# Two adaLN vector sums moved from the DeltaNet scan to the merge of its output, and the gate stores moved to ACT's queue

## The chip, the cores and the metric

The kernel runs on one core of one Trainium2 chip. The metric is the device time of one execution in microseconds (us). All arithmetic of the reference is float32.

## The reference

One block of a diffusion backbone, over 512 latent tokens and 256 context tokens of width 1024:

```
lat_mod = split(silu(c) @ w_mod + b_mod, 6)
h = rms_norm(x, norm1_g) * (1 + lat_mod[1]) + lat_mod[0]
merged = g_dn * (deltanet(h) @ w_proj_dn) + g_hy * (hyena(h) @ w_proj_hy) + g_lru * (rglru(h) @ w_proj_lru)
x = x + lat_mod[2] * (merged @ w_out)
h = rms_norm(x, norm2_g) * (1 + lat_mod[4]) + lat_mod[3]
x = x + lat_mod[5] * conv_ffn(h)
return rms_norm(x, final_norm_g)
```

The six vectors `lat_mod` (adaLN: shift, scale and gate of the two sub-layers) are a product of one row of 1024 numbers with a 1024 x 6144 matrix. This document is about vectors 2 to 5, called q = 0 to 3 in the kernel: q = 0 scales the output of the mixer, q = 1 and 2 shift and scale the input of the FFN, q = 3 scales its output. The gates g_dn, g_hy and g_lru, and the factor silu(z) of DeltaNet's output, are projections of h.

## The kernel before, in words

The block is one program for one core, and its parts follow each other: norm and modulation of the input, RG-LRU with its merge, queries, keys and values of DeltaNet, the triangular solves, **the scan** (12 steps over chunks of 64 tokens, both directions at once), then **the merge stage**: the first two groups of Hyena's input (`hy_in(0)`, L1143), the norm of DeltaNet's output (`dn_norm`, L1228), eight blocks `dn_merge(m)` (L1251) and Hyena's transform of its first quarter (`hy_fft(0)`, L1166) with its second input (`hy_in(1)`). Then come the rest of Hyena, the output projection and the FFN.

A matrix product is exact to float32 by three passes: each operand is split into a high and a low part, and `mm3` (L172) multiplies high by high (L173), high by low (L174) and low by high (L175). `load_w` (L164) loads a block of weights of 512 KB into a raw buffer (L168, on SP's queue), and `split` (L152) copies the high part (L155 on ACT or L157 on POOL) and subtracts it on DVE or POOL for the low part (L160). There are **three raw buffers** (ring `wr`, 4 KB of every partition each), two for high parts (`wh`) and two for low parts (`wl`), all at L148. Buffers go round: each call takes the next.

In the scan, PE's instructions are kept in the order of the program by `in_order((ET.PE,))` (L1114). A step (L996) subtracts what the state predicts (PE L1025, DVE L1029), applies the solved block (PE L1035, ACT L1037), updates the state (PE L1043, DVE L1048 in 16 pieces) and forms the output (PE L1055, ACT L1058 or DVE L1060). Between the halves of the steps stand 24 halves of 12 gate projections (`gate_halves`, L1091), whose results go through ACT (L594) to DRAM (L595, `gated`). POOL prepares the decayed queries and keys (L1012) from rows loaded at L1007.

Of the four adaLN vectors, `mod_part(q, k)` (L1068) loads 512 KB of w_mod into a raw buffer of the ring `wr` (L1070), multiplies it by c (a number per partition) and adds it to `acc` on DVE (L1072 for k = 0, L1074 for the other seven). `mod_sum(q)` (L1076) adds the partitions by matmuls against ones: eight of one column for q = 1 and 2 (L1080, DVE L1081), two of 512 columns for q = 0 and 3 (L1087, DVE L1088), which are then stored as a row to DRAM (`modr`). Eight products make a vector; in the loop L1103 four of them follow each of the steps 0, 1, 3, 4, 6, 7, 9 and 10, and the sums stand ahead of steps 2, 5, 8 and 11.

`dn_merge(m)` loads a block of `w_proj` by `load_w`, the gate (L1253, `gated[1, m]`) and what is merged so far (L1254, `mgd`), runs 24 matmuls of 512 columns, multiplies by the gate on DVE (L608), adds on POOL (L1256) and stores (L1257). The high part of its weights comes from POOL (L157), the low part from DVE (L160).

Outside the pinned stretches a list scheduler of the framework decides the order of the instructions on each engine and of the DMAs on each queue; engines and queues then run strictly in that order. SP issues nearly all DMAs and itself waits for the buffer that a DMA writes or for the data that it stores.

## Time and profile before

| | us |
|---|---|
| three runs | 2179.06, 1700.55, 1703.49 (median 1703.49) |
| profiled execution | 1699.04, of which 1696.9 span from the first to the last instruction |
| PE busy in the span | 1554.4 (92%) |
| DVE, ACT, POOL busy | 1202.8, 618.8, 587.0 |
| mean granted TensorE clock | 0.957 of full speed |

The sums of this document are made in the profiled execution and then set beside the runs. A matmul's recorded span overlaps that of the next, so a busy PE is not a PE at its peak, and what a change is worth is read from PE's idle time in the stage where it acts. "L160" is line 160 of the kernel before; because the diff takes a line away ahead of them, the lines L1070 to L1088 of `mod_part` and `mod_sum` are L1069 to L1087 after the change, and the merge stage's lines keep their numbers up to its loop.

### The profile page before, as it was taken

To read this page: it belongs to the slowest core of one execution; us is meant where nothing else is said; L and a number is where in the kernel's file an instruction comes from. 1 tells how busy PE (TensorE), PEld (TensorE's weight loads), DVE (VectorE), ACT (ScalarE), POOL (GpSimd) and SP (SyncE) were. 2 spreads that over 40 slices of the span, in tenths; PEclk is the share of its full clock that TensorE was granted. 3 is DMA by queue.
4 is the path that set the end of the run, shared out by engine and by line. 5 is a ranking of instruction groups with operands and counts; after the bars stand their busy time and mean duration, and the time that the engine had idled before them with its cause. 6 is when DMAs were issued, how large, how long until landed. Compare 5 with 4: busy or idle time off the path is not lost. (4 is left out here: it accounts for less than half of the span.)

```text
span 1696.9 us, 23679 instructions
## 1 busy us (share of the span) xinstructions
PE 1554.4 (92%) x9176; PEld 1264.1 (74%) x9176; DVE 1202.8 (71%) x1756; ACT 618.8 (36%) x1014; POOL 587.0 (35%) x407
## 2 busy tenths in 40 slices
PE   6989989889999988987899999999999999999998
PEld 1657767668787766875687777778878788888876
DVE  4677798765655999553675566777665899989873
ACT  3447878753454222231111150332222433333311
POOL 3752444433535351221333313222321234333441
PEclk7989999989999998788999999999999999999999
DMA  8522222234534332467889646322452123232331
GB/s 304 183 93 69 81 74 70 98 111 136 166 108 135 117 92 90 124 196 190 243 238 247 220 173 229 112 87 86 157 191 89 63 87 99 95 104 93 106 112 50
DMA packets 93057, 225.66 MB, mean 133 GB/s; under 512 B 9963, under 2 KB 30699, under 8 KB 92176
## 3 DMA queue, kind: packets, MB, share of 16 engines
q1 hardware_dynamic: 92112, 217.86, 40.9%
q0 software_dynamic: 832, 6.29, 0.9%
q8 instruction: 72, 1.18, 0.3%
q14 instruction: 41, 0.34, 0.1%
HBM read 190.45 MB, written 33.66 MB: 132 GB/s over the span
## 5 line engine op out<-in xcount | busy, mean ns | idle before, releaser
L173 PE MATMUL bank<-region,region 128*128 128x512 f32 (+1 forms) x2032 | 761.4, 376 | 23.8 <-DVE region L507 7.6
L175 PE MATMUL bank<-region,region 128*128 128x512 f32 (+1 forms) x2032 | 755.4, 373 | 24.6 <-DVE region L160 21.3
L174 PE MATMUL bank<-region,region 128*128 128x512 f32 (+1 forms) x2032 | 756.9, 373 | 5.0 <-DVE region L439 2.9
L173 PEld LDWEIGHTS bank<-region,region 128*128 128x128 f32 x2032 | 389.5, 192 | 101.6 <-ACT region L539 9.0
L175 PEld LDWEIGHTS bank<-region,region 128*128 128x128 f32 x2032 | 389.7, 192 | 97.7 <-DVE region L160 27.8
L174 PEld LDWEIGHTS bank<-region,region 128*128 128x128 f32 x2032 | 390.3, 192 | 69.6 <-DVE region L439 4.9
L160 DVE TENSOR_TENSOR region<-region,region 128x1024 fp32r<-128x1024 f32 (+2 forms) x241 | 269.8, 1133 | 173.0 <-ACT region L155 94.9
L155 ACT ACTIVATE region<-region 128x1024 fp32r<-128x1024 f32 (+2 forms) x209 | 178.4, 865 | 427.4 <-PE bank L174 130.0
L160 POOL TENSOR_TENSOR region<-region,region 128x1024 fp32r<-128x1024 f32 (+1 forms) x64 | 155.3, 2431 | 251.2 <-ACT region L155 210.8
L157 POOL TENSOR_SCALAR region<-region 128x1024 fp32r<-128x1024 f32 (+1 forms) x96 | 113.0, 1178 | 337.8 <-PE bank L174 151.2
L1443 DVE SCALAR_TENSOR_TENSOR region<-bank,pc,region 128x441 f32<-128x441 f32 (+2 forms) x352 | 224.8, 688 | 4.3 <-ACT region L1432 0.7
L505 DVE SCALAR_TENSOR_TENSOR region<-bank,pc,region 128x511 f32<-128x511 f32 (+1 forms) x56 | 34.1, 630 | 51.1 <-ACT region L502 47.3
L1074 DVE SCALAR_TENSOR_TENSOR region<-region,cc,region 128x1024 f32<-128x1024 f32 x28 | 42.1, 1504 | 35.9 <-DMA region<-in_w_mod_dram 35.5
L1012 POOL TENSOR_TENSOR region<-region,region 128x512 f32<-128x512 f32 x32 | 45.8, 1460 | 38.3 <-DMA region<-rowd 37.3
L502 ACT ACTIVATE region<-bank,pc 128x512 f32<-128x512 f32 (+1 forms) x40 | 23.0, 597 | 96.2 <-PE bank L175 96.2
L1455 POOL TENSOR_TENSOR region<-region,region 128x512 f32<-128x512 f32 x22 | 34.3, 1560 | 66.1 <-DVE region L1443 52.2
L1048 DVE SCALAR_TENSOR_TENSOR region<-region,egl,bank 128x128 f32<-128x128 f32 x160 | 42.3, 340 | 19.2 <-PE bank L1043 19.2
L1025 PE MATMUL bank<-region,region 128*64 128x128 f32 x608 | 38.9, 287 | 9.4 <-DVE region L1048 9.3
L1025 PEld LDWEIGHTS bank<-region,region 128*64 128x64 f32 x608 | 35.9, 145 | 14.6 <-DVE region L1048 6.3
L1037 ACT ACTIVATE region<-bank 128x512 f32<-128x512 f32 x24 | 14.3, 598 | 88.1 <-PE bank L1035 87.7
L594 ACT ACTIVATE region<-bank 128x512 f32<-128x512 f32 x32 | 18.8, 587 | 70.1 <-PE bank L175 66.0
L1035 PE MATMUL bank<-region,region 64*64 64x128 f32 x384 | 28.3, 298 | 12.7 <-DVE region L1029 6.9
(286 smaller groups left out, 1697.1 us busy)
## 6 DMA issues: line engine op xcount, KB each, us to landing
region<-in_w_in_dram SPq DMA_DIRECT2D x97, 512.0 KB, 3.6
region<-in_w_mod_dram SPq DMA_DIRECT2D x48, 512.0 KB, 6.7
region<-in_ffn_up_dram SPq DMA_DIRECT2D x44, 512.0 KB, 3.5
region<-in_w_proj_dram SPq DMA_DIRECT2D x24, 512.0 KB, 3.7
region<-in_ffn_down_dram SPq DMA_DIRECT2D x22, 512.0 KB, 3.4
gated<-region SPq DMA_DIRECT2D x32, 256.0 KB, 2.1
region<-gated SPq DMA_DIRECT2D x32, 256.0 KB, 3.5
kdd<-region SPq DMA_DIRECT2D x16, 384.0 KB, 2.8
```

The source lines that it names most:

```text
L155: act(hi, raw, AF.Copy)
L157: nc.gpsimd.tensor_scalar(hi, raw, 1.0, 0.0, op0=ALU.mult, op1=ALU.add)
L160: (vtt if e_lo == "dve" else gtt)(lo, raw, hi.bitcast(F32), op=ALU.subtract)
L173: mmul(ps, lh, rh, start=start, stop=False)
L174: mmul(ps, lh, rl, start=False, stop=False)
L175: mmul(ps, ll, rh, start=False, stop=stop)
L1012: gtt(wq[d][:, hs], KQ[hf][:, :, chs[d] - 4], eg[:, hs].unsqueeze(2).to_broadcast([P, 4, 2, 64]), op=ALU.mult)
L1025: mmul(X[hf][rcs[d], h, :], wq[d][:, hf * 4 + h, kind], S[d][:, hf * 4 + h, :], start=(kind == 0 or h == 0), stop=(kind == 0))
L1048: stt(S[d][:, h], S[d][:, h], egl[:, d, c, i, h:h + 1], p3[hf][d][:, h % 4], op0=ALU.mult, op1=ALU.add)
L1074: stt(acc, w_, cc[:, k, 0:1], acc, op0=ALU.mult, op1=ALU.add)
L1443: stt(uv[:, ro, co], pv_[:, ri, ci], w[:, a * 3 + b:a * 3 + b + 1], uv[:, ro, co], op0=ALU.mult, op1=ALU.add)
L1455: gtt(uu[0], uu[0], uu[1], op=ALU.mult)
```

## The change

The products and sums of q = 2 and 3 (16 loads of 512 KB, 16 DVE products, two sums) leave the scan and go into the loop over the eight blocks of the merge: two products behind each `dn_merge(m)`, the sum of q = 2 ahead of block 4, that of q = 3 behind block 7, with an accumulator `acc` of their own at 68 KB. In the scan two products stand behind each of the steps 0 to 3 and 6 to 9, and the sums ahead of steps 5 and 11. The store of a gate in the scan is issued from ACT's queue in place of SP's.

```diff
--- before.py
+++ after.py
@@ -589,10 +589,10 @@
     def load_gate(z_, m, e_hi="pool", e_lo="dve"):
         return load_w(I["w_in"][GATES[z_][0] + m], e_hi=e_hi, e_lo=e_lo)
 
-    def gate_store(z_, m, pg):
+    def gate_store(z_, m, pg, store=load):
         th = ur([P, NL])
         act(th, pg, GATES[z_][1])
-        load(gated[z_, m], th)
+        store(gated[z_, m], th)
 
     def gate(z_, m, e_hi="pool", e_lo="dve"):
         w = load_gate(z_, m, e_hi, e_lo)
@@ -1063,9 +1063,8 @@
 
     modr = dr.tile([2, D], F32, name="modr")
     mod34 = c1([P, 2, 8], "mod34")
-    acc = at(190, [P, D])
-
-    def mod_part(q, k):
+
+    def mod_part(acc, q, k):
         w_ = wr([P, D])
         load(w_, I["w_mod"][k * P:(k + 1) * P, (2 + q) * D:(3 + q) * D])
         if k == 0:
@@ -1073,7 +1072,7 @@
         else:
             stt(acc, w_, cc[:, k, 0:1], acc, op0=ALU.mult, op1=ALU.add)
 
-    def mod_sum(q):
+    def mod_sum(acc, q):
         if q in (1, 2):
             mp = mm([P, 8])
             for b in range(8):
@@ -1093,23 +1092,24 @@
         project_part(w, [(pg, hh, hl)], 0, 4)
         yield
         project_part(w, [(pg, hh, hl)], 4, 8)
-        gate_store(z_, m, pg)
+        gate_store(z_, m, pg, nc.scalar.dma_start)
         yield
 
     first_ins = len(bb.instructions)
     halves = (None for z_, m in fill[NFILL:] for _ in gate_halves(z_, m))
     ngap, FBM = 2 * (24 - NFILL), 1
     gap = 0
+    acc = at(190, [P, D])
     for s_ in range(12):
 
-        if s_ % 3 == 2:
-            mod_sum(s_ // 3)
+        if s_ % 6 == 5:
+            mod_sum(acc, s_ // 6)
         for part, _ in enumerate(step(s_)):
             gap += 1
             for _ in range(gap * ngap // 24 - (gap - 1) * ngap // 24):
                 next(halves)
-        for k in range(4) if s_ % 3 < 2 else ():
-            mod_part(s_ // 3, s_ % 3 * 4 + k)
+        for k in range(2) if s_ % 6 < 4 else ():
+            mod_part(acc, s_ // 6, s_ % 6 * 2 + k)
     assert next(halves, 1) == 1
     in_order((ET.PE,))
     dump("o", o)
@@ -1259,8 +1259,15 @@
 
     hin = hy_in(0)
     dn_norm()
-    for m in range(8):
+    acc = at(68, [P, D])
+    for m in range(9):
+        if m and m % 4 == 0:
+            mod_sum(acc, 1 + m // 4)
+        if m == 8:
+            break
         dn_merge(m)
+        for k in range(2):
+            mod_part(acc, 2 + m // 4, m % 4 * 2 + k)
         if m == FBM:
             nc.gpsimd.dma_start(fb, I["c_fwd"])
         if m == FBM + 1:
```

Three places show what that does to the order. In all rows region_902, region_440 and region_720 are the three raw weight buffers, region_721 and region_441 the two buffers for high parts, region_722 and region_442 those for low parts.

The first is DVE's queue in the merge stage, from the gate product (L608) of block 4 on. Before:

```order
L608 TENSOR_TENSOR region_1515<-region_1515,bank_64 128x512
L160 TENSOR_TENSOR region_722<-region_902,region_721 128x1024
L608 TENSOR_TENSOR region_974<-region_974,bank_65 128x512
L160 TENSOR_TENSOR region_442<-region_440,region_441 128x1024
L608 TENSOR_TENSOR region_1336<-region_1336,bank_63 128x512
L160 TENSOR_TENSOR region_722<-region_720,region_721 128x1024
```

Now, from the same gate product on (L1071 and L1073 are the products of `mod_part`, region_7297 is `acc`):

```order
L608 TENSOR_TENSOR region_1515<-region_1515,bank_65 128x512
L160 TENSOR_TENSOR region_722<-region_902,region_721 128x1024
L1071 TENSOR_SCALAR region_7297<-region_440,cc 128x1024
L1073 SCALAR_TENSOR_TENSOR region_7297<-region_720,cc,region_7297 128x1024
L160 TENSOR_TENSOR region_442<-region_902,region_441 128x1024
L608 TENSOR_TENSOR region_974<-region_974,bank_63 128x512
L1073 SCALAR_TENSOR_TENSOR region_7297<-region_440,cc,region_7297 128x1024
L1073 SCALAR_TENSOR_TENSOR region_7297<-region_720,cc,region_7297 128x1024
```

Before, the splits of three successive weight blocks read the three raw buffers in turn; now every one reads region_902, and the products read the other two. The gate product of block 5 now stands behind the split of block 7's weights.

The second place is SP's queue from the store of block 4's result (region_1515) to the end of the merge. Before:

```order
L1257 DMA mgd<-region_1515 128x512
L168 DMA region_902<-in_w_in_dram 128x1024
L1253 DMA region_2480<-gated 128x512
L1254 DMA region_1515<-mgd 128x512
L1257 DMA mgd<-region_974 128x512
L168 DMA region_440<-in_w_in_dram 128x1024
L1254 DMA region_974<-mgd 128x512
L1257 DMA mgd<-region_1336 128x512
L168 DMA region_720<-in_w_in_dram 128x1024
L1257 DMA mgd<-region_2480 128x512
```

Now, from the store of block 6's result (region_1336) on:

```order
L1257 DMA mgd<-region_1336 128x512
L1253 DMA region_2480<-gated 128x512
L1254 DMA region_974<-mgd 128x512
L1069 DMA region_440<-in_w_mod_dram 128x1024
L1069 DMA region_720<-in_w_mod_dram 128x1024
L1257 DMA mgd<-region_2480 128x512
L1083 DMA region_440<-in_b_mod_dram 1x1024
L168 DMA region_720<-in_w_in_dram 128x1024
```

Before, the gate of block 7 (the only L1253 of its piece) was issued ahead of the store of block 5's result, and the weights of `hy_in(1)` (in_w_in) stood among the blocks; now the gate of a block follows the store of the block before it, and the first weights of `hy_in(1)` stand behind the last store and in a buffer that the last product reads.

The third is PE's queue at the end of `hy_fft(0)` (bank_69). Before, `hy_in(1)` follows at once:

```order
L173 MATMUL bank_69<-region_7038,region_106 128x256
L174 MATMUL bank_69<-region_7038,region_106 128x256
L175 MATMUL bank_69<-region_7038,region_106 128x256
L173 MATMUL bank_65<-region_80,region_721 128x512
L174 MATMUL bank_65<-region_81,region_721 128x512
```

Now the sum of q = 3 (L1086) and two pieces of `hy_out(0)` (weights region_744) stand between:

```order
L174 MATMUL bank_69<-region_6991,region_106 128x256
L175 MATMUL bank_69<-region_6991,region_106 128x256
L1086 MATMUL bank_63<-region_7297,ones 1x512
L1086 MATMUL bank_64<-region_7297,ones 1x512
L173 MATMUL bank_67<-region_744,region_7869 128x256
L174 MATMUL bank_67<-region_744,region_7869 128x256
L173 MATMUL bank_68<-region_744,region_7869 128x256
L174 MATMUL bank_68<-region_744,region_7869 128x256
L173 MATMUL bank_65<-region_80,region_721 128x512
```

Of the 48 matmuls of 256 columns of `hy_fft(0)`, 21 are now spread over the blocks of the merge, and 27 stand between block 7 and L1086; before, all 48 stood behind block 7.

## Rows read from the trace of the kernel before

**Rows 1.** Busy time by stage: us; engines (instructions); granted clock; DMA share; GB/s
```profile
764.00:975.00 211.00, 183.88 (x1928) 151.58 (x1928) 118.11 (x236) 30.97 (x61) 62.62 (x50) 0.94 0.81 227
1030.00:1063.00 33.00, 32.37 (x143) 26.76 (x144) 17.36 (x13) 1.10 (x2) 13.29 (x11) 1.00 0.72 248
1063.00:1069.00 6.00, 6.00 (x51) 5.96 (x50) 5.59 (x7) 2.22 (x3) 1.29 (x1) 1.00 0.48 160
```

**Rows 2.** PE's waits in the scan, 780 to 970 us: total, times, longest
```profile
PE bank L1025 <- DVE region L1048: 9.3, 4, 5.9
PE bank L1035 <- DVE region L1029: 6.9, 5, 3.5
```

**Rows 3.** Timeline at scan step 3: start, us, engine, line [idle before <-releaser]
```profile
809.81 1.28 DVE L1074 SCALAR_TENSOR_TENSOR region<-region,cc,region 128x1024 f32<-128x1024 f32 x1
...
811.12 0.65 SPq L168 DMA_DIRECT2D region<-in_w_in_dram  x1
...
817.66 1.04 POOL L157 TENSOR_SCALAR region<-region 128x1024 fp32r<-128x1024 f32 x1 [5.12 <-DMA region<-in_w_in_dram]
818.74 1.22 DVE L160 TENSOR_TENSOR region<-region,region 128x1024 fp32r<-128x1024 f32 x1 [2.89 <-POOL region L157]
...
820.54 3.68 PE L1025 MATMUL bank<-region,region 128*64 128x128 f32 x32 [5.92 <-DVE region L1048]
```

**Rows 4.** Timeline of PE at the adaLN sums, and L1025 at scan step 2
```profile
800.12 1.02 PE L1087 MATMUL bank<-region,ones 128*1 128x512 f32 x2 [0.69 <-ACT region L594]
801.91 1.02 PE L1087 MATMUL bank<-region,ones 128*1 128x512 f32 x2 [0.77 <-DVE region L1088]
802.87 1.97 PE L1025 MATMUL bank<-region,region 128*64 128x128 f32 x32
...
853.08 1.95 PE L1080 MATMUL bank<-ones,region 128*128 128x1 f32 x16 [0.69 <-ACT region L594]
...
956.48 1.02 PE L1087 MATMUL bank<-region,ones 128*1 128x512 f32 x2 [0.69 <-ACT region L594]
959.24 1.53 PE L1087 MATMUL bank<-region,ones 128*1 128x512 f32 x2 [1.74 <-DVE region L1088]
```

**Rows 5.** Granted clock around the stall of step 3, columns as in the first group
```profile
802.80:804.80 2.00, 2.00 (x35) 1.75 (x34) 1.37 (x2) 0.00 (x0) 0.73 (x1) 1.00 0.49 127
820.50:824.30 3.80, 3.68 (x32) 3.28 (x32) 3.77 (x3) 0.00 (x0) 3.20 (x2) 0.50 0.76 195
```

**Rows 6.** SP's waits in the scan, 780 to 970 us
```profile
SPq L595 <- ACT region L594: 29.8, 10, 8.5
```

**Rows 7.** Timeline of one block of the merge: DVE, POOL and SP
```profile
1041.32 1.05 POOL L157 TENSOR_SCALAR region<-region 128x1024 fp32r<-128x1024 f32 x1 [1.54 <-issue]
1041.43 0.69 DVE L608 TENSOR_TENSOR region<-region,bank 128x512 f32<-128x512 f32 x1 [3.24 <-PE bank L175]
1042.34 1.28 POOL L1256 TENSOR_TENSOR region<-region,region 128x512 f32<-128x512 f32 x1
1042.41 2.30 DVE L160 TENSOR_TENSOR region<-region,region 128x1024 fp32r<-128x1024 f32 x1 [0.29 <-POOL region L157]
1044.29 0.36 SPq L1257 DMA_DIRECT2D mgd<-region  x1
1044.74 0.39 SPq L168 DMA_DIRECT2D region<-in_w_in_dram  x1
1046.88 0.69 DVE L608 TENSOR_TENSOR region<-region,bank 128x512 f32<-128x512 f32 x1 [2.17 <-PE bank L175]
```

**Rows 8.** DMAs issued in the merge, 1010 to 1066 us: KB each, median us to landing
```profile
region<-gated SPq DMA_DIRECT2D x12, 256.0 KB, 2.9
region<-in_w_proj_dram SPq DMA_DIRECT2D x4, 512.0 KB, 3.8
```

**Rows 9.** DMAs issued in the scan, 760 to 970 us
```profile
region<-in_w_mod_dram SPq DMA_DIRECT2D x27, 512.0 KB, 5.6
```

**Rows 10.** DVE's adaLN products: ns shortest, median, longest
```profile
L1074 DVE SCALAR_TENSOR_TENSOR region<-region,cc,region x28: 1272/1285/2267, 747.8 to 944.8; 128x1024 f32<-128x1024 f32 x28
```

## The prediction

> **What bounds the kernel now.** I read the page's slices first, then the busy time by stage, then, stage by stage, what PE waits for and the timeline there. By stage [rows 1], PE is busy 183.88 of 211 us in the scan, so some 27 us are idle, 5 of them at its start; DVE's 118.11 us show that the 16 products which leave were not too much work, only in the way. In the merge PE is busy 32.37 of 33 us: there is nothing to win there, and each wait that comes in is lost. So the change moves work from a stage with holes into a full one, and the question is which waits go and which come.
>
> In the scan PE waits 9.3 us for DVE's state update (L1048) and 6.9 us for its subtraction (L1029) [rows 2]. The longest of these, 5.92 us ahead of step 3, shows the mechanism [rows 3]: the adaLN product ends at 811.09, only then does SP issue the next gate's weights (811.12) into the buffer that it freed, POOL gets them at 817.66, DVE's split stands in its queue ahead of the last two update pieces and ends at 819.96, and PE goes on at 820.54. The two long matmul sums also hold PE up themselves [rows 4].
>
> **Gain in the scan.** (a) The sums. Before, with their waits: at step 2 0.69+1.02+0.77+1.02 = 3.50 us, at steps 5 and 8 0.69+1.95 = 2.64 each, at step 11 0.69+1.02+1.74+1.53 = 4.98 [rows 4] (the sum at step 8 read the same as that at step 5); 13.8 us. Now one of the first kind and one of the second stay, 6.1 us. Gain 7.6 us.
> (b) The waits for DVE, 9.3 + 6.9 = 16.2 us [rows 2]. With half the products, gate weights no longer share their raw buffer with a product, so the stall of rows 3 should go; those where the update merely stood behind products should shrink. But each split still stands ahead of a step's subtraction. I take two thirds, 11 us; bounds 3 and 16.2. A loss isn't excluded, since every gate's weights now use one buffer, but a gate is due only about every 17 us (211/12) and its load, 5.6 us in this stage [rows 9], fits.
> (c) The clock. Ahead of the stall the granted clock is 1.00 (2.4 GHz), after it 0.50 (1.2 GHz) [rows 5], and the same 32 matmuls take 3.68 us in place of 1.97 [rows 3, 4]. Some of that goes with the stalls: 2.6 us, bounds 0 and 4.3.
> (d) The gate stores. SP stands 29.8 us behind ACT's gate activation [rows 6] with the next step's loads behind it. That wait goes from SP; on ACT the store follows its own producer, and ACT is busy 30.97 of 211 us [rows 1], so it costs nothing there; if that cover failed, 12 issues of 0.4 us would come to 5 us. Its value is in (b), so 0 by itself.
> By the Trainium skill (DMA: Bandwidth & Descriptors, "Issuing engines are not separate DMA queues") a second issuing queue saves only issue time, usually small. Of 11 stores that would be 4 us of SP. Here the row shows waiting on the queue, not issue, as the larger part; by the rule alone (b) would stand nearer its lower bound.
> Sum: 7.6 + 11 + 2.6 = 21 us, bounds 6 and 28.
>
> **Loss in the merge.** A block takes 1046.88 - 1041.43 = 5.45 us now [rows 7].
> (e) The turn of one raw buffer. All w_proj blocks now use region_902, so block m+1 can be loaded only when m's split is done, and the split needs the landing. A turn is landing 3.8 us [rows 8] + POOL 1.05 + DVE 2.30 + 0.2 of hand-overs [rows 7] = 7.35; with two product loads beside it I take 4.05 for the landing: 7.6 us. Bounds: 6.2 with a split of 1.22 [rows 3], 9.2 with the scan's 5.6 [rows 9]. Blocks 0 to 2 have their weights in time. Five turns (blocks 3 to 7) at 7.6 - 5.45 come to 10.8 us; 21 of the transform's matmuls at 6.00/51 = 0.118 us [rows 1] fill 2.5 of that. 8.3 us, bounds 1.3 and 16.3.
> The transfers point the same way: 512 KB of weights, 3 x 256 KB and 2 x 512 KB of w_mod are 2.36 MB a block, and 248 GB/s at a share of 0.72 [rows 1] make 344 GB/s at a full one, or 6.9 us. By the Trainium skill (same page, "Specifications") the limit of HBM is about 358 GB/s per core, an estimate of 6.6 us a block: it speaks against the change, and the trace agrees to 4%.
> (f) The tail. The gate product of block 5 now stands behind the split of block 7's weights, the next gate is loaded only behind a store, and the last products behind that. From that split: L608 0.69, POOL 1.28, hand-overs 0.87, store 0.36 make 3.2 [rows 7]; gate 6 lands 2.9 + 0.1 later [rows 8]; another 3.2 to the store of block 6; 1.3 until both last products' loads are issued behind two others, 5.0 landing (3.8 with company), 1.28 for the last product [rows 10] and 0.2: 17.2 us. PE has block 7 (5.45) and 27 matmuls (3.2) meanwhile: it waits 8.5 us ahead of the sum of q = 3. Bounds: 2, if block 7's split isn't late (PE then has block 6 more), and 14 with the scan's landings.
> (g) The sums themselves: 1.95 and 2 x 1.02 = 4.0 us [rows 4], without a wait between the two, which have banks of their own.
> (h) The weights of `hy_in(1)`. Before, the first was issued at 1044.74 [rows 7], 24 us ahead of its use; now behind the last product, which reads its buffer: 3.8 landing [rows 8], 1.05 for the high part as in rows 7, 1.22 for the low part as in rows 3, hand-overs 0.4 are 6.5 us, of which the sum covers 2.3. 4.2 us, bounds 2 and 6.
> (i) The first of these two gaps is longer than the 5.92 us behind which the clock fell [rows 3, 5], the second shorter; that fall cost 3.68 - 1.97 = 1.7 us [rows 3, 4] and, as I estimate from the same ratio, 0.9 in what followed. 3.5 us for the two, bounds 0 and 5.5.
> The 16 products on DVE (1.29 us each [rows 10], 17.36 of 33 us busy [rows 1]) hide behind the turn; without that cover they would cost at most 21 us, which is inside the upper bounds of (e) and (f).
> Sum: 8.3 + 8.5 + 4.0 + 4.2 + 3.5 = 28.5 us, bounds about 10 and 46.
>
> **Total.** 28.5 - 21.2 = +7.3 us on the profiled execution of 1699.04: 1706.3. Of the runs shown, 1700.55 and the median of 1703.49 lie 3.0 above that execution on the mean, so I predict 1709, practically no change: 2% (34 us, about what a measurement of this kernel can tell from no change) is more than either side.
>
> **Rivals.**
> *The merge absorbs it.* Landings stay at 3.8 us, the splits are short because POOL's addition no longer falls beside them, and block 7's weights come in time: (e) 1.3, (f) 2, (g) 4, (h) 3, (i) 0 = 10 us against 28 in the scan: -18, 1684. For it: DVE and POOL have room in the merge. Against it: the 6.9 us of transfers a block.
> *The merge becomes bound by landings.* At 5.6 us and more, the turn of region_902 is 9.2 us: (e) 16.3, (f) 14, (g) 4, (h) 6, (i) 5.5 = 46 against 15 in the scan: +31, 1733, slower than before. It decides from a turn of about 8 us; over 2% from about 9.7. For it: the scan's landings at a share of 0.81; against: w_mod and w_proj rows are long, and small rows load the scan's queues.
> *The scan isn't freed.* The change doesn't do what it says: each step still waits for a split ahead of its subtraction, so only (a) is won. 28.5 - 7.6 = +21, 1723. For it: DVE's queue keeps the split there; against: the stall of rows 3 came from the buffer.
>
> **How the numbers follow.** The forecast (1700 to 1720) 0.42, absorbed 0.28, bound by landings 0.22, scan not freed 0.08. Range 1682 to 1736: it leaves out the outer part of the two outer cases, about 0.2. Slower by over 2% (1738) needs a turn near 10 us: 0.07. Faster by over 2% (1669) needs all of the scan's gain and no loss: 0.03. Within: 0.90.
>
> **What would show it.** In the profile after: PE's wait for L1048 at most a third of 9.3 us and no stall like that of step 3; SP's wait for the gate activation gone; gate products in the merge 7 to 8 us apart; a wait of PE of about 8 us ahead of the sum of q = 3 on the last product and a second ahead of `hy_in(1)`; the clock at 0.5 after them. Blocks still 5.45 us apart, or no wait ahead of that sum, would make (e) or (f) wrong; the scan as long as before less 8 us would make (b) wrong.

## The result, and the profile after

The changed kernel takes 1714.53 us (median of five runs, 1709.75 to 1715.42) against 1703.49 before: a ratio of 1.0058, 95% interval 1.0035 to 1.0082. That is about 10 us slower, inside the 2% that I called no change, and 5.5 us above the forecast of 1709. The sign was right, and the largest loss stands where I had put it. Both sides of the sum came out smaller than I had them: the scan gave 12.4 us in place of 21.2, and the merge took back 25.4 in place of 28.5.

First the stages of the changed kernel: stretch, busy time of PE, PEld, DVE, ACT and POOL, granted clock, DMA share, GB/s. They answer to [rows 1].

```profile
764.00:966.00 202.00, 179.40 (x1908) 150.42 (x1908) 95.39 (x216) 32.78 (x70) 61.93 (x50) 0.93 0.77 208
1021.00:1054.00 33.00, 31.22 (x145) 24.72 (x144) 20.48 (x19) 0.60 (x1) 12.20 (x9) 1.00 0.77 261
1054.00:1064.00 10.00, 10.00 (x59) 8.73 (x57) 7.12 (x8) 0.60 (x1) 2.73 (x3) 1.00 0.86 301
1064.00:1076.00 12.00, 0.34 (x2) 0.09 (x2) 11.02 (x11) 0.00 (x0) 6.57 (x4) 0.64 0.55 193
1076.00:1088.00 12.00, 9.71 (x25) 5.91 (x24) 9.35 (x13) 2.73 (x4) 2.31 (x2) 0.51 0.59 219
```

In the scan DVE lost 22.7 us of work and the stretch became 9 us shorter. In the merge PE stays busy until 1064, and then stands for 12 us with DVE busy 11 of them. After that gap the granted clock is about 0.5 (1.2 GHz) for the next 12 us, the sum and the first matmuls of `hy_in(1)` included.

PE's waits in the changed kernel's scan, 780 to 960 us (total, times, longest), answer to [rows 2]:

```profile
PE bank L1025 <- DVE region L1048: 7.3, 5, 3.6
PE bank L1035 <- DVE region L1029: 3.8, 3, 2.5
```

They are 11.1 us together, where they were 16.2. SP's longest waits in that stretch answer to [rows 6]. The wait of the store for ACT (L595) is gone, but SP stands as long for something else, the split that frees the one raw buffer of the gate weights:

```profile
SPq L168 <- DVE region L160: 34.5, 9, 10.4
SPq L993 <- PE bank L1043: 18.7, 6, 3.7
```

PE's waits in the changed kernel's merge, 1021 to 1084 us, and its timeline there. The whole merge has one large wait, and it is the one ahead of the sum of q = 3 (L1086):

```profile
PE bank L1086 <- DVE region L1073: 11.7, 1, 11.7
PE bank L173 <- ACT region L155: 2.3, 1, 2.3
```

```profile
1063.73 0.28 PE L175 MATMUL bank<-region,region 128*128 128x256 f32 x1
1075.67 3.57 PE L1086 MATMUL bank<-region,ones 128*1 128x512 f32 x4 [11.66 <-DVE region L1073]
1081.53 0.58 PE L173 MATMUL bank<-region,region 128*128 128x256 f32 x1 [2.29 <-ACT region L155]
```

What it waits for is two chains that meet in SP's queue, read off SP's and DVE's timelines of the changed kernel:

```profile
1058.15 0.43 SPq L1253 DMA_DIRECT2D region<-gated  x1
...
1060.96 0.69 DVE L608 TENSOR_TENSOR region<-region,bank 128x512 f32<-128x512 f32 x1 [0.38 <-DMA region<-gated]
...
1063.10 0.33 SPq L1257 DMA_DIRECT2D mgd<-region  x1
1063.47 0.43 SPq L1253 DMA_DIRECT2D region<-gated  x1
...
1064.98 1.28 DVE L1073 SCALAR_TENSOR_TENSOR region<-region,cc,region 128x1024 f32<-128x1024 f32 x1 [1.36 <-DMA region<-in_w_mod_dram]
...
1066.29 2.13 SPq L1069 DMA_DIRECT2D region<-in_w_mod_dram  x2
...
1066.78 1.28 DVE L1073 SCALAR_TENSOR_TENSOR region<-region,cc,region 128x1024 f32<-128x1024 f32 x1
...
1072.55 1.27 DVE L1073 SCALAR_TENSOR_TENSOR region<-region,cc,region 128x1024 f32<-128x1024 f32 x1
...
1074.34 1.27 DVE L1073 SCALAR_TENSOR_TENSOR region<-region,cc,region 128x1024 f32<-128x1024 f32 x1
1075.64 0.34 SPq L168 DMA_DIRECT2D region<-in_w_in_dram  x1
```

The gate of block 6 lands, is multiplied (1060.96), block 6 is stored (1063.10), and only behind that store does the gate of block 7 leave SP (1063.47). The loads of the last two products stand behind it in the queue, but SP was ready for them at 1064.4 and still waited: they left at 1066.29 and 1068.09, each as soon as the product before it had freed the raw buffer (1066.26 and 1068.06). That earlier pair had itself waited 1.36 us for its own loads. So the turn of the two buffers that the products use (load, landing, product, next load) releases the last loads. The last products run at 1072.55 and 1074.34, and only then is the first w_in block of `hy_in(1)` issued (1075.64).

Lengths worked out from the two traces (after minus before, first or last matmul of the lines named): up to the scan's first L1035 +2.7 (771.83 against 769.09); the scan, first L1035 to last L1055, -12.4 (190.5 against 202.9); from there to the norm of DeltaNet's output (first L1245) -0.2; from that norm to the second norm's first transpose (L1404, now L1411) +25.4 (326.4 against 301.0); the rest +0.3. That is +15.8, about the difference of the two profiled executions (1714.53 and 1699.04); the ratio over all runs makes 10 of it.

### The profile page after: what moved, and what is told of

The parts are those of the page before. It is cut to its first block, busy times and chain, and to the rows that moved or that the text cites. A ratio compares the mean times of both kernels' runs of the same rounds, so it can differ in the third digit from the quotient of the medians.

```text
span 1712.8 us, 23686 instructions
## 1 busy us (share of the span) xinstructions
PE 1566.6 (91%) x9176; PEld 1273.9 (74%) x9176; DVE 1189.9 (69%) x1756; ACT 618.7 (36%) x1014; POOL 588.7 (34%) x407
## 5 line engine op out<-in xcount | busy, mean ns | idle before, releaser
L175 PE MATMUL bank<-region,region 128*128 128x512 f32 (+1 forms) x2032 | 759.1, 375 | 24.3 <-DVE region L160 21.2
L175 PEld LDWEIGHTS bank<-region,region 128*128 128x128 f32 x2032 | 392.1, 193 | 98.2 <-DVE region L160 27.6
L160 DVE TENSOR_TENSOR region<-region,region 128x1024 fp32r<-128x1024 f32 (+2 forms) x241 | 263.3, 1105 | 179.2 <-ACT region L155 108.2
L1073 DVE SCALAR_TENSOR_TENSOR region<-region,cc,region 128x1024 f32<-128x1024 f32 x28 | 40.4, 1443 | 46.3 <-DMA region<-in_w_mod_dram 46.0
L1048 DVE SCALAR_TENSOR_TENSOR region<-region,egl,bank 128x128 f32<-128x128 f32 x160 | 42.2, 343 | 37.3 <-PE bank L1043 37.3
L1012 POOL TENSOR_TENSOR region<-region,region 128x512 f32<-128x512 f32 x32 | 44.6, 1417 | 39.6 <-PE bank L1025 23.6
L1462 POOL TENSOR_TENSOR region<-region,region 128x512 f32<-128x512 f32 x22 | 34.4, 1563 | 66.5 <-DVE region L1450 59.7
L1025 PE MATMUL bank<-region,region 128*64 128x128 f32 x608 | 39.6, 293 | 7.3 <-DVE region L1048 7.3
L1025 PEld LDWEIGHTS bank<-region,region 128*64 128x64 f32 x608 | 36.9, 148 | 11.6 <-DVE region L1048 7.4
L1157 POOL TENSOR_TENSOR region<-region,region 128x512 f32<-128x512 f32 x8 | 11.4, 1425 | 96.5 <-DVE region L1141 96.5
```

Of the source, the lines that this page charges most:

```text
L160: (vtt if e_lo == "dve" else gtt)(lo, raw, hi.bitcast(F32), op=ALU.subtract)
L175: mmul(ps, ll, rh, start=False, stop=stop)
L1012: gtt(wq[d][:, hs], KQ[hf][:, :, chs[d] - 4], eg[:, hs].unsqueeze(2).to_broadcast([P, 4, 2, 64]), op=ALU.mult)
L1025: mmul(X[hf][rcs[d], h, :], wq[d][:, hf * 4 + h, kind], S[d][:, hf * 4 + h, :], start=(kind == 0 or h == 0), stop=(kind == 0))
L1048: stt(S[d][:, h], S[d][:, h], egl[:, d, c, i, h:h + 1], p3[hf][d][:, h % 4], op0=ALU.mult, op1=ALU.add)
L1073: stt(acc, w_, cc[:, k, 0:1], acc, op0=ALU.mult, op1=ALU.add)
```

## The experiments

My theory when I began: the scan's gain is as found, and the loss is the chain of store, gate, landing and product with PE's program order. The rivals were the transfers (2.36 MB a block) and the shared raw buffer. The table gives what all kernels measured. "Scan" and "norm to norm" are the two lengths just defined, from the profiled execution; the ratio is to the kernel before, run beside on the same chip, with its interval. Of kernels with the same scan the length came out between 188 and 194 us, so differences below about 5 us in one profile say nothing.

| kernel | scan, us | norm to norm, us | median, us | ratio |
|---|---|---|---|---|
| before | 202.9 | 301.0 | 1703.49 | 1 |
| changed | 190.5 | 326.4 | 1714.53 | 1.0058 (1.0035 to 1.0082) |
| e1_sum_late | 188.1 | 326.7 | 1709.56 | 1.0049 (1.0028 to 1.0070) |
| e2_store_only | 212.8 | 300.1 | 1716.14 | 1.0079 (1.0037 to 1.0121) |
| e3_move_only | 198.1 | 328.7 | 1719.93 | 1.0114 (1.0065 to 1.0163) |
| e4_own_raw | 194.2 | 326.4 | 1713.87 | 1.0066 (1.0042 to 1.0090) |
| e5_q3_later | 190.8 | 318.4 | 1704.04 | 1.0017 (0.9998 to 1.0036) |
| e6_both_later | 193.3 | 316.2 | 1705.32 | 1.0030 (1.0008 to 1.0051) |
| e7_all_later | 173.3 | 343.5 | 1708.70 | 1.0046 (1.0025 to 1.0067) |
| e8_hyena_act_pool | 193.6 | 323.0 | 1714.13 | 1.0075 (1.0051 to 1.0099) |
| e9_small_loads | 190.9 | 316.2 | 1700.08 | 0.9986 (0.9962 to 1.0010) |
| e10_merge_act_pool | 190.9 | 335.4 | 1722.90 | 1.0136 (1.0116 to 1.0157) |
| e11_all_act_pool | 172.5 | 365.1 | 1728.74 | 1.0163 (1.0133 to 1.0192) |
| e12_two_early | 200.3 | 300.2 | 1718.38 | 1.0097 (1.0073 to 1.0120) |

**The sum behind `hy_in(1)`.**

```diff
-    for m in range(9):
-        if m and m % 4 == 0:
-            mod_sum(acc, 1 + m // 4)
-        if m == 8:
-            break
+    for m in range(8):
+        if m == 4:
+            mod_sum(acc, 2)
...
             hin = hy_in(qr + 1)
+            if qr == 0:
+                mod_sum(acc, 3)
```

> The changed kernel with only the sum of q = 3 moved: it stands behind hy_in(1) in the program and not ahead of it; its loads and products stay where they are. Theory (order in the tail: PE stands 11.7 us at that sum for the last product, and the w_in blocks of hy_in(1) wait for the same product's buffer): PE's gap ahead of the sum goes, hy_in(1) starts 9 to 14 us earlier, about 1702, at the level of the kernel before or below. Rival (transfers: 2.36 MB a merge block hold everything up): the wait only moves to hy_in(1)'s weights, which land as late as before, and the time stays at 1711 to 1715.

Measured: 1709.56, and the stretch from norm to norm is as long as in the changed kernel. PE's wait ahead of the sum went, but it came back, longer, one weight block on: PE ran the first block of `hy_in(1)` up to 1064.7 and then waited for the second. SP's and PE's timelines and the stage's row:

```profile
1073.77 2.13 SPq L168 DMA_DIRECT2D region<-in_w_in_dram  x2
...
1078.46 0.80 PE L173 MATMUL bank<-region,region 128*128 128x512 f32 x1 [13.71 <-ACT region L155]
```

```profile
1065.00:1078.50 13.50, 0.04 (x1) 0.04 (x1) 13.50 (x14) 1.74 (x2) 5.85 (x4) 0.67 0.70 226
```

The second block's load left SP at 1073.77, when a product had freed its raw buffer (the product ran from 1071.47 to 1073.75). So the sum's place was only what PE met first. DVE is busy for the whole 13.50 us, which made me suspect DVE's queue itself.

**Three raw buffers for the products alone.**

```diff
...
-    acc = at(68, [P, D])
+    acc, own = at(68, [P, D]), ring(4, [72, 60, 64])
...
-            mod_part(acc, 2 + m // 4, m % 4 * 2 + k)
+            mod_part(acc, 2 + m // 4, m % 4 * 2 + k, own)
```

> The changed kernel with three raw buffers of their own for the products of the merge, at 72, 60 and 64 KB, so that w_proj's blocks have the three shared ones again; the sum stays ahead of hy_in(1). Theory (the tail hangs on the order of stores, gates and product loads in SP's queue and on the shared ring): the blocks of the merge come 5.5 us apart again, the products are loaded early, PE's 11.7 us ahead of the sum shrink to 0 to 4, hy_in(1)'s weights are early too: about 1700. Rival (transfers: the same 2.36 MB a block): the blocks stay at 6.3 us or more and the gap moves, 1710 or more.

Measured: 1713.87, nothing gained. PE's and SP's timelines:

```profile
1070.11 0.77 PE L173 MATMUL bank<-region,region 128*128 128x512 f32 x1 [6.66 <-DVE region L608]
```

```profile
1057.96 0.33 SPq L1257 DMA_DIRECT2D mgd<-region  x1
1058.34 0.42 SPq L1253 DMA_DIRECT2D region<-gated  x1
...
1065.23 0.33 SPq L1257 DMA_DIRECT2D mgd<-region  x1
1065.61 0.42 SPq L1253 DMA_DIRECT2D region<-gated  x1
...
1072.84 0.33 SPq L1257 DMA_DIRECT2D mgd<-region  x1
```

With the buffers free, the product loads no longer wait, and the other chain holds: store, next gate, landing, gate product, store, 7.3 and 7.6 us a turn, where a block took 5.45 before [rows 7]. PE now waits for a gate product (L608), whose result bank it needs, in place of a product. So the shared buffers are not all that sets the tail: the two chains are about equally long, and taking away one of them leaves the other.

**Loads of 64 KB in place of 512.**

```diff
-        load(w_, I["w_mod"][k * P:(k + 1) * P, (2 + q) * D:(3 + q) * D])
+        n = D if q < 2 or k == 0 else P
+        load(w_[:, 0:n], I["w_mod"][k * P:(k + 1) * P, (2 + q) * D:(2 + q) * D + n])
```

> The changed kernel with the 14 loads of the merge's products after the first of each vector cut from 512 to 64 KB (128 of 1024 columns), so those two vectors are not computed from the right data; every instruction, wait and buffer stays. Theory (order in DVE's and SP's queues): the products still stand where they stood, but their loads land some 2 to 3 us sooner, so that PE's 11.7 us shrink only to 6 to 9: about 1709 to 1712. Rival (transfers: 2.36 MB a block): a block has 1.4 MB, the blocks come 5.5 us apart, the wait of 11.7 us is gone or under 3 us, about 1700.

The kernel leaves out 896 of 1024 columns of these blocks, so two vectors are not the right ones; only its time is of use. Measured: 1700.08, the rival's number, though from norm to norm it is still 15.2 us longer than before. PE's waits from 1018 to 1074 us, and SP's timeline (one line down: L1254 is the gate's load here, L1258 the store):

```profile
PE bank L173 <- ACT region L155: 3.2, 1, 3.2
...
PE bank L1087 <- DVE region L1074: 0.9, 1, 0.9
```

```profile
1047.09 0.42 SPq L1254 DMA_DIRECT2D region<-gated  x1
...
1059.29 0.33 SPq L1258 DMA_DIRECT2D mgd<-region  x1
1059.72 0.99 SPq L1070 DMA_DIRECT2D region<-in_w_mod_dram  x2
...
1066.01 0.34 SPq L1258 DMA_DIRECT2D mgd<-region  x1
1066.44 0.38 SPq L168 DMA_DIRECT2D region<-in_w_in_dram  x1
```

The wait ahead of the sum is 0.9 us with all products still on DVE and in the same ring. So the gap comes from the loads and not from the length of DVE's work. But not the edit alone acted: the list scheduler, reckoning with small loads, also issued the gate of block 7 at 1047.09, ahead of the stores of blocks 5 and 6, where the changed kernel has it behind one at 1063.47. Shorter landings (w_mod 2.3 in place of 4.7 us, a median over 1000 to 1090 us of each) and the earlier gate came together, and I can't part them.

**The products of the merge on ACT and POOL.** ACT multiplies a block by its scalar, POOL adds it to `acc`.

```diff
...
-            stt(acc, w_, cc[:, k, 0:1], acc, op0=ALU.mult, op1=ALU.add)
+            act(w_, w_, AF.Copy, scale=cc[:, k, 0:1])
+            gtt(acc, acc, w_, op=ALU.add)
```

> The changed kernel with its 16 products in the merge, but on ACT (times the scalar) and POOL (the addition), with the same loads, buffers and sums. Theory (DVE's queue is the cause in the tail): DVE is not busy throughout PE's wait, the blocks come 5.5 us apart and the wait ahead of the sum falls to about 5, which is the chain of stores, gates and loads: about 1706. Rival (chain of loads and transfers alone): the wait stays at 10 us or more, because POOL's addition of 1024 columns comes on top, 1713 or more.

Measured: 1722.90, a ratio of 1.0136 where the changed kernel has 1.0058. Waits of 3.0, 8.3 and 3.4 us stand in the tail. An addition took POOL 2.54 us (median of 14), 2.8 in the tail, and POOL is busy 8.31 of the 9.00 us of the longest wait:

```profile
1072.00:1081.00 9.00, 0.72 (x4) 0.25 (x2) 7.80 (x5) 0.64 (x2) 8.31 (x5) 0.69 0.34 92
```

The second theory, that the products cost by their place in DVE's queue, didn't hold here: off DVE they cost more. As an addition is about twice as long on POOL, this alone doesn't clear DVE's queue.

**One vector, then both, in the Hyena loop.** The products go one at a time behind the groups of `hy_in`, `hy_out` and (for two vectors) `hy_fft`; `parts` is a generator of a vector's eight products and its sum, `parts(3)` in the first of the two kernels.

```diff
...
+            if qr:
+                next(late, 0)
...
+    late = parts(2, 3)
...
```

> The changed kernel with the whole vector q = 3 (eight loads, eight products, the sum) taken out of the merge and spread over hy_in(1) to hy_out(2), one product at a time; q = 2 stays in blocks 0 to 3. In e1_sum_late DVE was busy all 13.5 us of PE's wait, with products ahead of the split of hy_in(1)'s weights. Theory now (the tail's loss is the products that stand in DVE's queue there): the wait behind the merge goes, hy_in(1) starts as in the kernel before or earlier, the Hyena loop takes the products in DVE's 30% of idle time: about 1697, 12 to 18 us below the changed kernel. Rival (the 2.36 MB a block in blocks 0 to 3 are enough to delay the merge): hy_in(1) still starts over 5 us late, 1706 or more. Second rival (the Hyena loop has no room either: its DVE is busy 0.7): the loop gets longer by about the 10 us that the products took, about 1710.

> The changed kernel with both vectors, q = 2 and q = 3, spread over the Hyena loop (16 products, two sums), none in the merge. Theory: the scan keeps its gain of 12 us, the merge takes its 33 us as in the kernel before, the loop grows by the sums' 4 us and little else: about 1693, below both kernels. Rival (the loop has no room): its PE waits at the transforms grow by 10 us or more, 1703 or more.

Measured: 1704.04 and 1705.32. Both are level with the kernel before to within 0.3%, neither is shown to be below it. With both vectors out of the merge, from norm to norm it is still 15.2 us longer than before. PE's waits from 1021 to 1330 us of e6_both_later, against 7.2 and 3.9 us for the same two in the kernel before:

```profile
PE bank L175 <- DVE region L160: 9.3, 6, 2.7
PE bank L1161 <- POOL region L1157: 8.5, 5, 3.2
```

These are 6.7 us more of waiting; the sums and a lower granted clock make the rest, since PE's busy time from norm to norm grew by 9.0 us (295.9 against 286.9). So e5's second rival was nearer in its mechanism, though its 1710 was not: the loop has little room.

**Both in the loop, on ACT and POOL.** (The edit is that of e6_both_later with that of the merge, above.)

> As e6_both_later (q = 2 and q = 3 in the Hyena loop), but ACT multiplies each block by its scalar and POOL adds it to the sum, so that DVE has no part in the 16 products. In e6_both_later the stretch from the norm to the second norm was 15.3 us longer than in the kernel before, although DVE's share in that loop is about 0.7. Theory (a product costs by its place in DVE's queue, wherever it stands): the loop loses only the sums' 4 us and a little of the shared port, about 1695. Rival (the loads of w_mod, 512 KB each in the buffers that w_in uses, are what delays the loop): no change against e6_both_later, 1703 to 1707.

Measured: 1714.13. It is 6.8 us worse than with DVE from norm to norm. That is neither the theory nor the rival, which expected no change.

**No product in the scan.**

```diff
-        for k in range(2) if s_ % 6 < 4 else ():
-            mod_part(acc, s_ // 6, s_ % 6 * 2 + k)
...
-    late = parts(2, 3)
+    late = parts(0, 1, 2, 3)
```

> All four vectors in the Hyena loop, two products at each place, none in the scan. It shows what the scan is worth without any product: PE's waits there for DVE were 11.1 us in the changed kernel. Theory (the products are what is in the way in the scan): those waits fall below 4 us and the scan is 6 to 10 us shorter than the changed kernel's. Rival (each gate's split ahead of a step's subtraction is the cause): the scan stays within 3 us of the changed kernel's. The loop with 32 products is expected to lose: 1695 to 1715 in all.

Measured: the scan is 17.2 us shorter than the changed kernel's, twice what I had, and PE's waits for DVE are 6.7 us, not below 4. PE's waits from 775 to 942 us:

```profile
PE bank L1035 <- DVE region L1029: 5.2, 3, 3.0
PE bank L1025 <- DVE region L1048: 1.5, 3, 0.6
```

Both readings have a part. The products had caused 4.4 of the 11.1 us, and the splits ahead of the subtraction keep most of L1029's waits alive. From norm to norm it loses 42.5 us, so 1708.70 in all.

> As e7_all_later (all four vectors in the Hyena loop, two products at each place), with the products on ACT and POOL. Without a product the scan took 173.3 us there against 190.5 in the changed kernel, and the loop lost 42.5 against the kernel before, for 32 products. Theory (DVE's queue): the scan keeps its 173 us and the loop loses the sums' 8 us and some 10 of POOL's additions and shared port: about 1690, below the kernel before. Rival (loads and buffers): the loop loses as much as in e7_all_later, about 1707.

With the same products on ACT and POOL: 1728.74, and 64 us lost from norm to norm. A clear miss.

**The two edits of the change apart.** The first takes only the stores to ACT's queue, the second only moves the products:

```diff
...
-        gate_store(z_, m, pg)
+        gate_store(z_, m, pg, nc.scalar.dma_start)
```

```diff
-        gate_store(z_, m, pg, nc.scalar.dma_start)
+        gate_store(z_, m, pg)
```

> The kernel before with only the gate stores of the scan moved to ACT's queue. Theory (the store's move is worth little by itself, as PE's waits in the scan come from DVE's queue and from the buffer that products and weights share): SP's 29.8 us behind ACT go, the scan gets 0 to 3 us shorter, about 1700 to 1703. Rival (most of the 12.4 us that the scan won came from the stores, because SP is free to issue the next step's loads): the scan gets 6 to 10 us shorter, about 1694.

> The changed kernel with the scan's gate stores back on SP's queue. Theory (stores worth little): the scan is within 3 us of the changed kernel's, the merge as there, about 1713 to 1717. Rival (stores worth most of the scan's gain): the scan is 6 to 10 us longer than the changed kernel's, about 1722.

Measured, for the scan: stores alone 9.9 us longer than before, move alone 4.8 shorter (within what two profiles of one scan can differ by), both 12.4 shorter. The edits don't add. With the stores alone, another 5.3 us went between the scan and the norm. All 32 products are still in the scan there, and the scheduler's new order puts some of them ahead of a step's work: PE's waits for the subtraction rose from 6.9 to 13.7 us. DVE's and PE's timelines of e2_store_only show one such place:

```profile
882.41 2.23 DVE L1074 SCALAR_TENSOR_TENSOR region<-region,cc,region 128x1024 f32<-128x1024 f32 x1 [5.02 <-DMA region<-in_w_mod_dram]
884.57 2.28 DVE L160 TENSOR_TENSOR region<-region,region 128x1024 fp32r<-128x1024 f32 x1
...
886.77 1.27 DVE L1029 TENSOR_TENSOR region<-region,bank 128x512 f32<-128x512 f32 x2
887.50 2.83 PE L1035 MATMUL bank<-region,region 64*64 64x128 f32 x24 [4.97 <-DVE region L1029]
```

A product waits 5.02 us for its block, and a split and the subtraction L1029 stand behind it. At the same step of the kernel before, DVE had run the subtraction at 872.44 and the next product only at 878.96. With the move made and the stores on SP, the queue shows it. PE's and SP's waits of e3_move_only, 780 to 962 us:

```profile
PE bank L1025 <- DVE region L1048: 13.9, 6, 4.5
```

```profile
SPq L595 <- ACT region L594: 43.3, 10, 14.1
```

There SP stands 43.3 us behind ACT, and PE waits 13.9 us for the update where it waited 7.3 with the stores on ACT. e3's rival expected this (6 to 10 us of scan); that the stores alone would cost 9.9 us, neither theory nor rival of e2 did. The kernel's loss is clear of noise (1.0037 to 1.0121). The 7.6 us are less sure: 198.1 us lie 4 us above the range of the kernels with the changed scan, and the ratio's interval (1.0065 to 1.0163) overlaps the changed kernel's; the waits are the better evidence.

**Two vectors ahead of the scan.** If any place had room, I thought, it is the loop over the LRU merge and the queries.

```diff
+    own, acc = ring(4, [156, 160]), at(152, [P, D])
+    early = parts(0, 3)
...
         lru_merge(h)
+        next(early, 0)
         if h < 6:
             sqs.append(query(h + 2))
+        next(early, 0)
...
```

> The vectors q = 0 and q = 3 move into the loop over the LRU merge and the queries (around 380 to 490 us of the kernel before, where DVE is busy 60 of 100 us and the DMA share is 0.47), one product at each of three places a turn, with an accumulator and two raw buffers of their own; q = 1 and q = 2 stay in the scan at the changed kernel's pace, with the gate stores on ACT; none in the merge. Theory (two vectors less in the scan are worth 12 us; what two cost elsewhere depends on whether that stage has DMA, DVE and buffers to spare): the early loop grows by the two sums' 4 us and up to 4 more, the merge takes its time of before: about 1698. Rival (two vectors cost 15 to 25 us in any place behind or ahead of the scan, as they did in the merge and in the Hyena loop): 1705 or more.

Measured: 1718.38. The merge and the Hyena loop are as before (300.2), which confirms from the other side that their loss came from the products. But the scan begins at 792.0 in place of 769.1, so two vectors cost 22.9 us there, the rival's price. PE stands in the new place too; its timeline:

```profile
470.75 0.79 PE L173 MATMUL bank<-region,region 128*128 128x512 f32 x1 [6.11 <-ACT region L155]
```

Its scan took 200.3 us with the same count of products and the same queue for the stores as the changed kernel. PE's waits for the update and the subtraction are 17.3 us there, no less than the 16.2 of the kernel before. Why it isn't 190 stays open, and with it how much of the 12.4 us half the products and the queue of the stores are worth in another schedule. No version beat the kernel before by more than the intervals.

## Why the prediction came out right

- **(a) The sums in the scan**, 7.6 forecast: 6.0. What stays is 0.69 + 1.02 + 0.77 + 1.02 = 3.50 at the first sum and 1.46 + 2.86 = 4.32 at the second, which ran at a lower clock than I had (2.86 in place of 1.95 us); 13.8 less 7.8.
- **(b) PE's waits for DVE**, 11 forecast: 16.2 - 11.1 = 5.1. The wait for L1048 fell to 7.3 us and not to a third of 9.3. This is the step most wrong on the gain's side. I took two thirds because a gate's load fits into its 17 us. But the split still stands ahead of the step's work, and e7_all_later shows 6.7 us of it without any product at all. The rival "the scan isn't freed" was half right.
- **(c) The clock in the scan**, 2.6: the other terms leave 1.3 us of the 12.4, but nothing shows them to be the clock's, as the granted clock of the scan was 0.95 before (769 to 975 us) and 0.95 after (772 to 966).
- **(d) The stores**, "0 by itself": wrong as a statement by itself, since alone they lost 9.9 us of scan; right in saying that their value shows only in (b). By the Trainium skill (DMA: Bandwidth & Descriptors, "Issuing engines are not separate DMA queues") the second queue saves issue time only. The pair e3_move_only and changed kernel points to more (7.6 us of scan, against the 4 us of issue in the prediction), with SP's wait of 43.3 us behind ACT as the reason, but the 3.6 us between these two numbers are less than two profiles of one scan can differ by.
- **The start of the scan**, not in the sum: +2.7, a longer wait for the first vd load (7.86 against 5.32). The profiles with products in the scan, but fewer of them, show 6.2 to 7.9 there, those with none or all thirty-two 5.3. I have no cause for it.
- **(e) The turn of one raw buffer**, 8.3 forecast: 1.9. The first L175 of block 2 came 8.67 us earlier than before (1021.96 against 1030.63), the transform ended 4.8 earlier (1064.0 against 1068.8): 3.9 us lost, of which the sum of q = 2 is 1.95. The term of the turn that was too large is DVE's split. I took 2.30 us; from block 2 on five of six splits took 1.21 to 1.23, as "the merge absorbs it" had said. So the w_proj loads left SP about 6.45 us apart, near my lower bound of 6.2, save for 8.2 us at the sum of q = 2; PE had the transform's matmuls to fill in meanwhile. The gate products came 5.3 to 11.6 us apart, but not by this turn: those of blocks 5 and 6 waited for their gates to land. DVE's and SP's timelines:

```profile
1033.71 1.23 DVE L160 TENSOR_TENSOR region<-region,region 128x1024 fp32r<-128x1024 f32 x1 [2.69 <-POOL region L157]
...
1034.96 0.33 SPq L168 DMA_DIRECT2D region<-in_w_proj_dram  x1
...
1041.30 0.33 SPq L168 DMA_DIRECT2D region<-in_w_proj_dram  x1
```

- **(f) The tail**, 8.5 forecast: 11.66. From the end of block 7's split (1055.41) to the store of block 6 it took 8.0 us where I had 9.4, and the landing and the last product took 7.2 where I had 6.5. The link that was wrong lies between them: from that store until both loads had left SP, 5.0 us in place of 1.3. I had them standing behind two other loads; they waited for the products that held their two buffers, a turn that the prediction didn't count. The transform's pointwise work, which DVE ran without a pause between the last gate product and the last two products (L1184 to L1193, 1068.57 to 1072.6), added at most about 1.5 us: by the merge's median landing of 4.7 us the last block was there at about 1072.8, an estimate, and its product ran at 1074.34.
- **(g) The sums in the merge**, 4.0: 1.95 + 3.57 = 5.5, since the second ran behind the gap at half the clock; the 1.7 us that this cost (1.88 at full clock in e9_small_loads) are of the kind that (i) was to hold.
- **(h) The weights of `hy_in(1)`**, 4.2: a second wait came, 2.3 us, but not for them. PE waits there for the first operand of `hy_out(0)`, whose high part ACT makes at 1080.85, behind the transform's pointwise work on POOL. The high part of the weights was ready at 1082.42, 3.2 us behind the sum's end (1079.24) and just ahead of the first matmul that needs it (1082.56), so most of my 4.2 us was there, behind another wait. ACT's timeline (the first of the three is that operand, the second the weights):

```profile
1080.85 2.10 ACT L155 ACTIVATE region<-region 128x512 fp32r<-128x512 f32 x3 [17.64 <-POOL region L1195]
```

- **(i) The clock behind these gaps**, 3.5: 4.0 us are left of the 25.4. Of these 1.2 were lost ahead of block 2, and 2.7 are a longer wait further on (4.54 us in place of 1.81 ahead of the transposes L1161), so beside the 1.7 in (g) no row gives the clock a share.

So the sign held because the merge's loss was larger than the scan's gain. That the total came out near the forecast is in part luck, as the errors partly cancelled: 8.8 us less gain in the scan, 3.1 less loss in the merge, 2.7 at the scan's start and 0.1 elsewhere moved the sum from +7.3 to +15.8 in the profiled pair. In the merge the 3.1 are themselves the sum of errors both ways: (e) was 6.4 us too large, (f) 3.2 too small. The rule by the HBM limit (the Trainium skill, same page, "Specifications", about 358 GB/s per core) spoke against the change, and e9_small_loads, whose edit takes away only bytes, agrees that the loads matter; but its 6.6 us a block isn't what PE waited for, as PE was busy 31.22 of 33 us until 1054.

**What is shown and what isn't.** Shown: the scan won 12.4 us and the merge gave back twice that. The merge's loss comes from the moved products with their loads: PE's gap goes when the loads get small (e9) or when q = 3 leaves the merge (e5, e6), the whole loss when both vectors go ahead of the scan (e12). It only moves with another place of the sum (e1), with other buffers (e4) or with other engines (e10). Not parted: long landings, which both chains hold, and the order of the gates behind the stores, as no run changed one without the other. Not shown: what the scan's gain is due to, since e12 has the changed scan's edits and not its waits.

## What to carry to other kernels

A wait on a queue is removed only if what stands next in that queue is early. With in-order queues and a list scheduler, price two edits together and apart: here one lost 10 us alone and won about 8 with the other. Work that is spread over a stage pays at that stage's end: follow store, next load, landing and next store to the last block, follow each ring of buffers in the same way, and count the turn of the longer chain, not the busy share. Taking away one of two chains of equal length wins nothing. And when a thing costs something wherever it is put, moving it wins little at best. Here a vector cost 6.2 and 8.6 us in the scan (half of 202.9 - 190.5, which has the move of the stores in it, and of 190.5 - 173.3), 7.6 in the Hyena loop (half of 15.2), 12.7 in the merge (half of 25.4) and 11.5 ahead of the scan (half of 22.9).

## What the runs showed of the hardware

- Behind a wait of 11.66 us PE's granted clock was 0.50 (1.2 GHz): the sum of q = 3 took 3.57 us there, and 1.88 at a granted clock of 1.00 (2.4 GHz) in e9_small_loads, where PE had waited 0.9 us.
- In slices of about 1.1 us the changed kernel's merge moved up to 389 GB/s, more than the 358 which that section of the Trainium skill's page (DMA: Bandwidth & Descriptors, "Specifications") gives as a core's limit; one core ran alone here. This is the row of GB/s in 40 slices from 1021 to 1064 us:

```profile
GB/s 0 42 198 320 379 204 274 290 240 366 339 284 309 181 316 389 351 271 278 160 286 316 229 332 381 297 65 122 358 250 286 377 375 347 90 288 373 232 320 309
```

So the mean of 301 GB/s in the block ahead of the gap was not a ceiling, and that sentence of the prediction ("the trace agrees to 4%") read a mean as a limit.
- POOL's addition of 128x1024 in e10_merge_act_pool took 2.35 to 3.38 us (median 2.54), against 1.28 us for DVE's multiply and add of the same shape [rows 10].
- DVE's split of 128x1024 took 2.30 us in the kernel before, where POOL's addition of 128x512 had started 0.07 us ahead of it [rows 7]. At 1048.29 us of the changed kernel the split started 0.16 us ahead of the addition: there the split took 1.21 us, and the addition 2.20 in place of 1.29.
